# A three-layer transformer kernel: the first token tile's split moves into the output projection, and the first expert gather is cut in two

## The chip, the cores and the metric

The kernel runs on one core of a Trainium2 chip. The metric is the time of one execution on the device in microseconds (us). TensorE (PE) multiplies matrices, VectorE (DVE), ScalarE (ACT) and GpSimd (POOL) work on elements, and SyncE (SP) issues most of the transfers. Each engine works through its own instructions in the order in which the program issues them.

## The reference, cut to what matters

Three layers, each a token mixer and a mixture of experts, over 256 tokens of 1024 numbers in float32. The change lies between the mixer's output projection and the first expert product:

```python
x = x + gate1 * y                                  # y: the mixer's output projection
h = _rms(x, norm2_w[layer]) * (1 + scale2) + shift2
x = x + gate2 * _hier_moe(h, ...)

# in _hier_moe
g_sel = jnp.argmax(g_logits, axis=-1)              # 4 groups of 8 experts
top_v, top_i = lax.top_k(e_in, MOE_TOPK)           # 2 experts of the group
gate = (p_g * jax.nn.softmax(top_v, axis=-1)).reshape(-1)
def expert_block(args):
    tok, e = args
    xr = xt[tok]
    return (jax.nn.silu(xr @ w1[e]) * (xr @ w3[e])) @ w2[e]
```

The third layer's expert part is of the same kind, without shift, scale and gate. All 32 experts of a layer are computed, each for the tokens routed to it.

## The kernel before

The 256 tokens are two tiles of 128 (`t` = 0 and 1). All weights come through a ring of 18 slots of 1 MB. A plan fixes their order; `pump` issues the next transfer on SP while more slots are free than `self.reserve` holds back, `slot` takes one for data (and lowers the reserve by one), and `release` gives slots back, may raise the reserve, and pumps.

A mixer's last step is `out_last`: for each tile, two halves of 512 columns are projected on TensorE, and `out_sink` multiplies by the gate (first two layers) and adds to `x` on DVE, then ACT squares the half and sums it into `ssq`. While tile 1 is projected, tile 0 is transposed into `hT` (`route_turn`, copies on ACT and on DVE) and its router logits are multiplied (`route_logits`).

`moe` begins the routing. `x_rstd` sums `ssq` for both tiles at once, and `rstd` raises it to -0.5 on POOL. Then come `route_turn(1)` and `route_logits(1)`. ACT scales both tiles by `r` into `hh`, whose type float32r keeps the high part of each number. The low part `hl` is the scaled x less `hh`: for tile 0 POOL makes it in two steps (scaling into a scratch, then the subtraction), for tile 1 `rest` makes it in one DVE step.

`route` forms the logits `lg` and picks group and experts in a chain of small DVE steps, which ends with the mask `mk`. In the first two layers the late modulation products (`mods`) lie beside it on TensorE. `warm(n)` multiplies constants n times, only to keep TensorE busy. A product over `mk` counts ranks, `rk`. `onehot(0)` compares the ranks with 0 to 63 for four experts, `finish` makes the weights and the largest rank, and `gather(0)` multiplies `hh` and `hl` by the one-hot `u`, 256 columns for the two pairs 0 and 1 (two experts a pair); `affine` evacuates to `xg`, on ACT and DVE in turn. Every engine then reads the largest rank and branches around `overflow`.

The pairs follow: `up` with the first weights (`g`), `up` with the second (`u`), the turn, `down`, and `combine` of the pair before. After odd pairs the next two pairs are gathered.

Of the kernel before, what the change touches and what calls it, by code (L numbers as in the profile page):

```python
# [9 lines left out]
FT = mybir.dt.float32  # L10
# [9 lines left out]
P = 128  # L20
# [101 lines left out]
class Net:  # L122
# [396 lines left out]
    def out_last(self, act, gate):  # L519
        got = []  # L520
        setup = self.route_setup()
        next(setup)
        self.hT = self.slot().rearrange("p (k q) -> p k q", k=KC)
        for t in range(NT):
            for n in range(2):
                p = self.psum()
                for k2 in range(2):
                    i = 2 * n + k2
                    if i == len(got):
                        self.prep()  # L530
                        got.append(self.ready.pop(0))
                    wh, wl = got[i]
                    for k in range(2):
                        kk = 2 * k2 + k
                        self.mm3(p, tuple(x[:, P * t:P * t + P] for x in act[kk]), (wh[:, k], wl[:, k]), kk == 0, kk == 3)
                    yield (1.3, 0.0)
                self.out_sink(t, n, gate, True)(p)
                if not t and not n:
                    next(setup)
                if t:  # L540
                    (self.route_logits if n else self.route_turn)(0)
                    yield (1.8, 0.0)

# [124 lines left out]
    def gla(self, g, q):  # L668
# [116 lines left out]
        self.release(4, reserve=1)  # L785
# [83 lines left out]
    def even(self, coeffs):  # L869
# [91 lines left out]
        self.release(5, reserve=2)  # L961
# [16 lines left out]
    def odd(self, coeffs):  # L978
        nc, A, tc = self.nc, self.A, self.tc
        with tc.tile_pool(name="odd", bufs=1, reuse_waits="tile") as g:  # L980
# [77 lines left out]
            def stream():  # L1058
# [18 lines left out]
                self.release(3, reserve=1)  # L1077
# [4 lines left out]
        self.release(6, reserve=2)  # L1082
# [354 lines left out]
    def second(self, coeffs):  # L1437
        nc, tc = self.nc, self.tc
        with tc.tile_pool(name="sec", bufs=1, reuse_waits="tile") as g:
# [98 lines left out]
            def stream():  # L1538
# [23 lines left out]
                self.release(3, reserve=1)  # L1562
# [7 lines left out]
        self.release(6, reserve=2)  # L1570
# [58 lines left out]
    def route(self, g, r, mods, rest):  # L1629
# [5 lines left out]
        self.warm(1 if mods else 5)  # L1635
# [31 lines left out]
        rest()  # L1667
# [4 lines left out]
        self.warm(1)  # L1672
# [91 lines left out]
    def moe(self, l, mods, start, coeffs, slots, fill=None):  # L1764
        nc, tc = self.nc, self.tc
        _, w1, w3, w2, gate = self.moe_args(l)
        with tc.tile_pool(name="moe", bufs=1, reuse_waits="tile") as g:
            hT = self.hT
            hh, hl = (self.slot(FR).rearrange("p (t k q) -> p t k q", t=NT, k=KC) for i in range(2))
            r = self.x_rstd()  # L1770
# [3 lines left out]
            for t in range(NT):  # L1774
                nc.scalar.activation(hh[:, t], xv[:, t], AF.Copy, scale=r[:, t:t + 1])
            h0 = g.tile([P, KC, 2 * P], FT, name="xg").rearrange("p (t k) q -> p t (k q)", t=NT)[:, 0]
            h0 = h0.rearrange("p (k q) -> p k q", k=KC)
            nc.gpsimd.tensor_scalar(h0, xv[:, 0], r[:, 0:1], None, op0=OP.mult)
            nc.gpsimd.tensor_sub(hl[:, 0], h0, hh[:, 0].bitcast(FT))

            def rest():
                nc.vector.scalar_tensor_tensor(hl[:, 1], xv[:, 1], r[:, 1:2], hh[:, 1].bitcast(FT),
                                               op0=OP.mult, op1=OP.subtract)
# [20 lines left out]
            def gather(j):  # L1804
                xg = g.tile([P, KC, 2 * P], FT, name="xg")
                u = st["u", j].rearrange("p t a s -> p t (a s)")
                for k0 in range(0, KC, 2):
                    ps = self.psum().rearrange("p (k s) -> p k s", k=2)
                    for k in range(2):
                        for t in range(NT):  # L1810
                            for i, part in enumerate((hh, hl)):
                                self.mm(ps[:, k], part[:, t, k0 + k], u[:, t], t + i == 0, t + i == 2)
                    for k in range(2):
                        self.affine(xg[:, k0 + k], ps[:, k], k0 + k, "av"[k])
                st["xg"] = xg
# [108 lines left out]
            onehot(0)  # L1924
            finish()
            gather(0)
# [6 lines left out]
            for p in range(NP):  # L1933
# [13 lines left out]
                else:  # L1947
# [9 lines left out]
                    up(p, "u")  # L1957
                    if p % 2:
# [107 lines left out]
```

## Time and profile before

| | |
|---|---|
| median of 3 runs | 2107.69 us (2103.13 to 2118.58) |
| profiled execution, its own time | 2108.36 us |
| its span, first to last instruction | 2106.3 us |
| TensorE busy | 1901.6 us (90%) |
| DVE / ACT / POOL busy | 858.1 / 427.5 / 327.9 us |
| mean granted TensorE clock | 0.968 |
| read from memory | 722.48 MB, 344 GB/s over the span |

Times in the trace are counted from the span's start. A busy time is a sum over one engine and says nothing of what waits for what; for that the timeline is read around a wait. The granted clock is a share of 2.4 GHz. An arrow in square brackets gives an engine's idle time before an instruction and what ended it.

### The profile page before, as it was taken

What the parts mean: (1) busy time and instruction counts of PE and PEld (TensorE: products, weight loads), DVE (VectorE), ACT (ScalarE), POOL (GpSimd) and SP (SyncE); (2) the same over time, 40 slices, a digit from 0 to 9 for tenths busy, and PEclk for the clock granted to TensorE, in tenths of its full rate; (3) what the DMA queues carried; (4) which work ended last, traced back from release to release, by engine and by line L of the source; (5) the groups of instructions that cost most, each with busy time, mean ns of one, the idle gap of its engine ahead of it and who ended that gap; (6) DMA issues with size and microseconds to landing.
All of it is one profiled execution on the core that took longest, in us unless ns stands there. A gap on an engine that the chain in (4) does not pass through costs nothing. (4 is left out here: it accounts for less than half of the span.)

```text
span 2106.3 us, 24926 instructions
## 1 busy us (share of the span) xinstructions
PE 1901.6 (90%) x9930; PEld 1056.1 (50%) x9930; DVE 858.1 (41%) x1574; ACT 427.5 (20%) x778; POOL 327.9 (16%) x248
## 2 busy tenths in 40 slices
PE   6888799999999899899999999998899899999997
PEld 3656344444444667534444444586788344444443
DVE  3665333333322567533332232467666333232223
ACT  1423101111100343211110011254544111010011
POOL 1331100000000334100000000142444000000000
PEclk8998899999999999999999999998999999999999
DMA  9697799999999856799999999921357799999997
GB/s 323 238 319 297 260 422 421 422 421 421 421 421 406 300 222 244 294 365 421 421 421 421 421 421 421 326 101 41 125 194 300 292 421 421 421 421 422 421 421 285
DMA packets 157547, 725.35 MB, mean 344 GB/s; under 512 B 25305, under 2 KB 43088, under 8 KB 85226
## 3 DMA queue, kind: packets, MB, share of 16 engines
q1 hardware_dynamic: 139216, 716.84, 84.9%
q10 hardware_dynamic: 18201, 6.76, 1.3%
q8 instruction: 85, 1.39, 0.3%
q14 instruction: 45, 0.36, 0.0%
HBM read 722.48 MB, written 1.07 MB: 344 GB/s over the span
## 5 line engine op out<-in xcount | busy, mean ns | idle before, releaser
L257 PE MATMUL ps<-slot,xg 128*64 128x512 f32 x2992 | 710.5, 599 | 20.6 <-DMA slot<-moe_w 9.6
L257 PEld LDWEIGHTS ps<-slot,xg 128*64 128x64 f32 x2992 | 254.4, 138 | 422.0 <-issue 359.8
L257 PE MATMUL ps<-slot,ht 128*64 128x512 f32 (+1 forms) x1552 | 345.0, 574 | 56.4 <-issue 49.2
L257 PE MATMUL ps<-slot 128*128 128x256 f32 (+8 forms) x2230 | 368.4, 327 | 15.1 <-DVE slot L461 9.6
L257 PEld LDWEIGHTS ps<-slot 128*128 128x128 f32 (+3 forms) x2230 | 300.5, 187 | 73.6 <-issue 14.0
L257 PEld LDWEIGHTS ps<-slot,ht 128*64 128x64 f32 x1552 | 128.7, 139 | 228.4 <-issue 213.9
L1891 DVE TENSOR_TENSOR x<-x,ps 128x512 f32<-128x512 f32 x180 | 115.3, 682 | 277.0 <-PE ps L257 277.0
L1865 POOL TENSOR_TENSOR yl<-sg,yh 128x512 fp32r<-128x512 f32 (+1 forms) x68 | 82.5, 1213 | 884.8 <-ACT yh L1864 884.8
L462 POOL TENSOR_TENSOR slot<-slot 128x512 fp32r<-128x512 f32 (+2 forms) x108 | 164.4, 1539 | 273.2 <-ACT slot L460 261.9
L1844 DVE SCALAR_TENSOR_TENSOR hh<-sg,ws,ps 128x512 f32<-128x512 f32 x48 | 53.4, 1113 | 319.4 <-PE ps L257 179.8
L1864 ACT CAST yh<-sg 128x512 fp32r<-128x512 f32 (+1 forms) x68 | 40.3, 593 | 468.9 <-DVE sg L1863 468.9
L461 DVE TENSOR_TENSOR slot<-slot 128x512 fp32r<-128x512 f32 (+2 forms) x108 | 110.2, 1035 | 54.4 <-ACT slot L460 53.9
L1863 DVE TENSOR_TENSOR sg<-ps,ga 128x512 f32<-128x512 f32 (+1 forms) x68 | 44.9, 660 | 175.2 <-PE ps L257 175.2
L460 ACT CAST slot<-slot 128x1024 fp32r<-128x1024 f32 (+2 forms) x108 | 106.6, 1020 | 46.2 <-PE ps L257 27.3
L257 PEld LDWEIGHTS ps<-u,slot 128*128 128x128 f32 x768 | 96.9, 199 | 18.3 <-issue 17.0
L257 PE MATMUL ps<-u,slot 128*128 128x256 f32 x768 | 101.9, 293 | 0.0
L1840 ACT ACTIVATE sg<-ps 128x512 f32<-128x512 f32 x48 | 28.7, 598 | 312.4 <-PE ps L257 312.4
L257 PE MATMUL ps<-yh,pg 128*128 128x512 f32 (+1 forms) x204 | 87.1, 429 | 0.7 <-ACT yh L1864 0.7
L257 PE MATMUL ps<-yl,pg 128*128 128x512 f32 (+1 forms) x204 | 77.5, 382 | 0.9 <-POOL yl L1865 0.8
L1916 POOL TENSOR_TENSOR slot<-x,rows 128x512 f32<-128x512 f32 x2 | 2.5, 1272 | 464.5 <-DVE x L1912 464.5
L398 ACT ACTIVATE xg<-ps,cf 128x256 f32<-128x256 f32 x64 | 36.2, 565 | 156.6 <-PE ps L257 156.6
L1867 ACT CAST yh<-ps 128x512 fp32r<-128x512 f32 (+1 forms) x34 | 19.1, 561 | 227.3 <-PE ps L257 227.2
(334 smaller groups left out, 1586.4 us busy)
## 6 DMA issues: line engine op xcount, KB each, us to landing
slot<-moe_w SPq DMA_DIRECT2D x376, 1024.0 KB, 19.8
slot<-w_gate SPq DMA_DIRECT2D x59, 1024.0 KB, 17.7
slot<-w_up SPq DMA_DIRECT2D x59, 1024.0 KB, 19.8
slot<-w_down SPq DMA_DIRECT2D x50, 1024.0 KB, 18.1
slot<-ada_w SPq DMA_DIRECT2D x48, 1024.0 KB, 7.7
slot<-w_in SPq DMA_DIRECT2D x20, 1024.0 KB, 8.5
slot<-odd_w_in SPq DMA_DIRECT2D x12, 1024.0 KB, 13.1
more<-w_down SPq DMA_DIRECT2D x10, 1024.0 KB, 19.8
```

What stands on the lines that cost most here:

```text
L257: self.nc.tensor.matmul(out, lhsT=lhsT, rhs=rhs, start=start, stop=stop)
L398: self.nc.scalar.activation(out, p, AF.Identity, scale=a, bias=nb[:, k:k + 1])
L460: nc.scalar.copy(wh, src)
L461: nc.vector.tensor_sub(wl[:, 0], src[:, 0], wh[:, 0].bitcast(FT))
L462: nc.gpsimd.tensor_sub(wl[:, 1], src[:, 1], wh[:, 1].bitcast(FT))
L1840: nc.scalar.activation(sg, ps, AF.Silu)
L1844: nc.vector.scalar_tensor_tensor(ha.rearrange("s k p -> s p k"), st["sg", p].rearrange("s (p k) -> s p k", k=4), st["ws", p], ps.rearrange ...
L1863: nc.vector.tensor_mul(y, ps, self.ga[:, sl])
L1864: nc.scalar.copy(yh, y)
L1865: nc.gpsimd.tensor_sub(yl, y, yh.bitcast(FT))
L1867: nc.scalar.copy(yh, ps)
L1891: nc.vector.tensor_add(self.x[:, t, sl], self.x[:, t, sl], ps)
```

## The change

A new `token_split(t)` is called in `out_last` after each tile's second half. It sums and raises the tile's own `ssq`, scales the tile into `hh` on ACT, and for tile 0 makes `hl` on POOL, with the part of `hT` that belongs to tile 1 as scratch. `moe` no longer does this; its `x_rstd`, both scalings and the POOL steps are gone. The two slots for `hh` and `hl` are taken at the start of `out_last`, and the reserves are raised before it and dropped after it accordingly (five places; the hunks left out are of the kind shown). `rest` makes the low part of tile 1 in two halves, one at its old place and one after `onehot(0)`. The first gather makes only the 128 columns of pair 0; those of pair 1 follow after pair 0's second `up`. `warm` goes from 5 to 7 (layer 2) after the logits and from 1 to 2 after the rank product.

```diff
--- before.py
+++ after.py
@@ -521,6 +521,8 @@
         setup = self.route_setup()
         next(setup)
         self.hT = self.slot().rearrange("p (k q) -> p k q", k=KC)
+        self.hs = [self.slot(FR).rearrange("p (t k q) -> p t k q", t=NT, k=KC) for i in range(2)]
+        self.hr = self.cp.tile([P, NT], FT, name="xr", bufs=2)
         for t in range(NT):
             for n in range(2):
                 p = self.psum()
@@ -537,9 +539,24 @@
                 self.out_sink(t, n, gate, True)(p)
                 if not t and not n:
                     next(setup)
+                if n:
+                    self.token_split(t)
                 if t:
                     (self.route_logits if n else self.route_turn)(0)
                     yield (1.8, 0.0)
+
+    def token_split(self, t):
+        nc = self.nc
+        r = self.hr[:, t:t + 1]
+        nc.vector.tensor_reduce(r, self.ssq[:, t, :2], axis=AX.X, op=OP.add)
+        self.rstd(r, r, D)
+        hh, hl = self.hs
+        xv = self.x[:, t].rearrange("q (p k) -> q k p", k=KC)
+        nc.scalar.activation(hh[:, t], xv, AF.Copy, scale=r)
+        if t == 0:
+            f = self.hT[:, :, P:]
+            nc.gpsimd.tensor_scalar(f, xv, r, None, op0=OP.mult)
+            nc.gpsimd.tensor_sub(hl[:, t], f, hh[:, t].bitcast(FT))
 
     def plan_cols(self, key, w, c0, n):
         src = w.rearrange("(p k) n -> p k n", k=KC)[:, :, c0:c0 + n]
@@ -782,7 +799,7 @@
                        p.rearrange("p (h q) -> p h q", h=4))
             yield (0.9, 0.0)
         self.flag("ob", 1.5)
-        self.release(4, reserve=1)
+        self.release(4, reserve=3)
 
     def swa(self, g, bias, sc):
         nc, A = self.nc, self.A
@@ -1632,7 +1649,7 @@
         for t in range(NT):
             nc.vector.scalar_tensor_tensor(lg[:, t], self.lp[:, t], r[:, t:t + 1], self.br, op0=OP.mult, op1=OP.add)
         late = self.mods(mods[0][0], mods[0][1], (0, 1)) if mods else None
-        self.warm(1 if mods else 5)
+        self.warm(1 if mods else 7)
         gl = lg[:, :, 0:4]
         el = lg[:, :, 4:36]
 
@@ -1664,12 +1681,12 @@
         ob = g.tile([P, NT, 8], FT, name="ob")
         nc.vector.tensor_add(ob, o1, o2)
         nc.vector.tensor_mul(v4(mk), gb, r4(ob))
-        rest()
+        rest(0)
         p = self.psum((P, NT, E))
         self.mm(p[:, 0], self.ltri, mk[:, 0], True, True)
         self.mm(p[:, 1], self.ones, mk[:, 0], True, False)
         self.mm(p[:, 1], self.ltri, mk[:, 1], False, True)
-        self.warm(1)
+        self.warm(2)
         rk = g.tile([P, NT, E], FT, name="rk")
         nc.vector.scalar_tensor_tensor(rk, p, 1.0, mk, op0=OP.add, op1=OP.mult)
         nc.vector.tensor_scalar(rk, rk, -1.0, None, op0=OP.add)
@@ -1766,21 +1783,14 @@
         _, w1, w3, w2, gate = self.moe_args(l)
         with tc.tile_pool(name="moe", bufs=1, reuse_waits="tile") as g:
             hT = self.hT
-            hh, hl = (self.slot(FR).rearrange("p (t k q) -> p t k q", t=NT, k=KC) for i in range(2))
-            r = self.x_rstd()
+            hh, hl = self.hs
+            r = self.hr
             self.route_turn(1)
             self.route_logits(1)
             xv = self.x.rearrange("q t (p k) -> q t k p", k=KC)
-            for t in range(NT):
-                nc.scalar.activation(hh[:, t], xv[:, t], AF.Copy, scale=r[:, t:t + 1])
-            h0 = g.tile([P, KC, 2 * P], FT, name="xg").rearrange("p (t k) q -> p t (k q)", t=NT)[:, 0]
-            h0 = h0.rearrange("p (k q) -> p k q", k=KC)
-            nc.gpsimd.tensor_scalar(h0, xv[:, 0], r[:, 0:1], None, op0=OP.mult)
-            nc.gpsimd.tensor_sub(hl[:, 0], h0, hh[:, 0].bitcast(FT))
-
-            def rest():
-                nc.vector.scalar_tensor_tensor(hl[:, 1], xv[:, 1], r[:, 1:2], hh[:, 1].bitcast(FT),
-                                               op0=OP.mult, op1=OP.subtract)
+            def rest(k):
+                nc.vector.scalar_tensor_tensor(hl[:, 1, k:k + 4], xv[:, 1, k:k + 4], r[:, 1:2],
+                                               hh[:, 1, k:k + 4].bitcast(FT), op0=OP.mult, op1=OP.subtract)
 
             rk, wt, ti, finish, late = self.route(g, r, mods, rest)
             NP = E // 2
@@ -1801,18 +1811,19 @@
                 nc.vector.tensor_mul(uw, u, bc(wt, 2 * p, 2))
                 st["uw", p] = uw
 
-            def gather(j):
-                xg = g.tile([P, KC, 2 * P], FT, name="xg")
+            def gather(j, c=slice(0, 2 * P)):
+                if c.start == 0:
+                    st["xg"] = g.tile([P, KC, 2 * P], FT, name="xg")
+                xg = st["xg"]
                 u = st["u", j].rearrange("p t a s -> p t (a s)")
                 for k0 in range(0, KC, 2):
-                    ps = self.psum().rearrange("p (k s) -> p k s", k=2)
+                    ps = self.psum().rearrange("p (k s) -> p k s", k=2)[:, :, :c.stop - c.start]
                     for k in range(2):
                         for t in range(NT):
                             for i, part in enumerate((hh, hl)):
-                                self.mm(ps[:, k], part[:, t, k0 + k], u[:, t], t + i == 0, t + i == 2)
+                                self.mm(ps[:, k], part[:, t, k0 + k], u[:, t, c], t + i == 0, t + i == 2)
                     for k in range(2):
-                        self.affine(xg[:, k0 + k], ps[:, k], k0 + k, "av"[k])
-                st["xg"] = xg
+                        self.affine(xg[:, k0 + k, c], ps[:, k], k0 + k, "av"[k])
 
             def gather_w(p):
                 ps = self.psum((P, T))
@@ -1922,8 +1933,9 @@
                 add(3)
 
             onehot(0)
+            rest(4)
             finish()
-            gather(0)
+            gather(0, slice(0, P))
             if late is not None:
                 late()
             self.pump()
@@ -1955,6 +1967,8 @@
                             nc.scalar.dma_start(fw, self.A["final_norm_2"].rearrange("(o n) -> o n", o=1)
                                                 .to_broadcast([P, D]))
                     up(p, "u")
+                    if not p:
+                        gather(0, slice(P, 2 * P))
                     if p % 2:
                         gather(p // 2 + 1)
                         if p == NP - 3:
```

## Rows read from the trace of the kernel before

**Rows 1.** Windows by stretch: length, busy time of each engine, granted clock, DMA share, rate.

```profile
core 0: us, PE busy (x) PEld busy (x) DVE busy (x) ACT busy (x) POOL busy (x), PEclk, DMA share, GB/s
220.00:225.00 5.00, 4.42 (x20) 4.00 (x21) 2.87 (x16) 0.95 (x4) 0.00 (x0) 0.50 0.70 290
225.00:230.00 5.00, 2.28 (x16) 2.08 (x15) 3.01 (x6) 1.72 (x4) 0.00 (x0) 0.84 0.04 10
250.00:260.00 10.00, 8.30 (x40) 2.83 (x38) 2.46 (x5) 0.00 (x0) 0.00 (x0) 1.00 0.81 252
300.00:400.00 100.00, 93.99 (x462) 41.30 (x460) 32.76 (x50) 10.61 (x18) 7.67 (x6) 1.00 1.01 421
```

**Rows 2.** Timeline of layer 0's routing: start, length, engine, line, operation.

```profile
201.45 0.19 ACT L382 ACTIVATION_READ_ACCUMULATOR junk<-x 128x1 f32 x1
...
206.50 0.69 DVE L508 TENSOR_TENSOR x<-x,junk 128x512 f32<-128x512 f32 x1
...
207.99 0.59 ACT L248 COPY slot<-ps 128x512 f32<-128x512 f32 x1
208.04 0.16 DVE L387 TENSOR_REDUCE xr<-ssq 128x2 f32<-128x4 f32 x1 [0.85 <-ACT junk L382]
...
208.48 0.70 POOL L378 TENSOR_TENSOR xr<-xr,mhalf 128x2 f32<-128x2 f32 x1 [15.81 <-DVE xr L377]
...
208.63 1.98 PE L257 MATMUL ps<-wr,slot 128*128 128x36 f32 x16 [0.23 <-ACT slot L248]
209.21 4.22 ACT L1775 ACTIVATE slot<-x,xr 128x1024 fp32r<-128x1024 f32 x2 [0.63 <-POOL xr L378]
209.28 3.87 POOL L1778 TENSOR_SCALAR xg<-x,xr 128x1024 f32<-128x1024 f32 x1
...
210.53 3.64 PE L257 MATMUL ps<-slot,condz 128*32 128x512 f32 x32
210.71 0.42 DVE L1633 SCALAR_TENSOR_TENSOR lg<-ps,xr,br 128x36 f32<-128x36 f32 x2 [1.58 <-PE ps L257]
...
213.23 2.35 POOL L1779 TENSOR_TENSOR slot<-xg,slot 128x1024 fp32r<-128x1024 f32 x1
...
217.25 2.06 DVE L1782 SCALAR_TENSOR_TENSOR slot<-x,xr,slot 128x1024 fp32r<-128x1024 f32 x1
...
221.09 6.19 PE L257 MATMUL ps<-u,slot 128*128 128x256 f32 x32
...
231.44 9.40 PE L257 MATMUL ps<-slot,xg 128*64 128x512 f32 x32 [4.15 <-issue]
```

**Rows 3.** Timeline of layer 1: the first gather and the first expert product.

```profile
871.05 5.54 PE L257 MATMUL ps<-u,slot 128*128 128x256 f32 x32
...
879.37 7.09 PE L257 MATMUL ps<-slot,xg 128*64 128x512 f32 x32 [2.78 <-DVEq L1717]
```

**Rows 4.** Timeline of layer 2's routing.

```profile
1617.72 0.18 ACT L382 ACTIVATION_READ_ACCUMULATOR junk<-x 128x1 f32 x1
...
1625.68 1.98 PE L257 MATMUL ps<-wr,slot 128*128 128x36 f32 x16 [0.23 <-ACT slot L248]
...
1627.49 4.24 PE L257 MATMUL ps<-km 128*128 128x476 f32 x10
...
1638.04 5.99 PE L257 MATMUL ps<-u,slot 128*128 128x256 f32 x32
...
1645.85 7.09 PE L257 MATMUL ps<-slot,xg 128*64 128x512 f32 x32 [1.82 <-DVEq L1717]
```

**Rows 5.** One source line's instructions: shortest, median and longest in ns.

```profile
L1649 DVE TENSOR_TENSOR oh<-km,i x6: 174/176/2083, 213.5 to 1633.6; 128x16 f32<-128x16 f32 x6
```

**Rows 6.** Timeline of TensorE over pairs 0 and 1 of layer 0.

```profile
252.97 0.66 PE L267 MATMUL ps<-km,hh 128*128 128x128 f32 x4 [0.91 <-DVE hh L1844]
...
276.43 4.00 PE L257 MATMUL ps<-u,slot 128*128 128x256 f32 x32
```

**Rows 7.** Groups by shape from 1345 to 1385 us on TensorE: count, busy us.

```profile
L257 PE MATMUL ps<-slot 128*128 128x152 f32 x36 | 4.5, 274 | 0.0
```

**Rows 8.** The branch around the overflow code on TensorE's sequencer, in ns.

```profile
L1717 PEldq COMPARE_BRANCH  x3: 3578/3798/3818, 224.9 to 1641.6; - x3
```

More of the change, by code (lines that the diff above doesn't have):

```diff
@@ L960, in even @@
                        stream())
-        self.release(5, reserve=2)
+        self.release(5)
     def plan_odd(self):
@@ L1076, in stream @@
                 yield tuple(("o", h) for h in range(4, 8))
-                self.release(3, reserve=1)
+                self.release(3, reserve=3)
                 yield from self.out_last([(self.o[0][:, h], self.o[1][:, h]) for h in range(4, 8)], True)
@@ L1081, in odd @@
             self.weave(*[transposed(s) for s in (2, 0, 3, 1)], *[head(h) for h in range(8)], stream())
-        self.release(6, reserve=2)
+        self.release(6)
     def plan_second(self):
@@ L1561, in stream @@
                 yield from branch(self.o[2:], 1)
-                self.release(3, reserve=1)
+                self.release(3, reserve=3)
                 coeffs()
@@ L1569, in second @@
             self.weave(self.nsa_prep(g), self.nsa_attn(g, sc), self.hgrn(g, q8), stream())
-        self.release(6, reserve=2)
+        self.release(6)
     def plan_moe(self, l):
```

## The prediction

> **What bounds the kernel now.** I read the windows by stage first. In the expert stages the weight stream and TensorE are both nearly full: between 300 and 400 us TensorE works 94 of 100 us while the DMA engines move 421 GB/s without a gap [rows 1]. So nothing can be won inside such a stage; what can move are its two ends. The start is visible in the same view: from 225 to 230 us the DMA engines move 10 GB/s, because the ring is full and TensorE has not yet used a weight, and from 250 to 260 us they are again below their rate, because the ring is still full before the first pair's last product [rows 1]. A microsecond by which TensorE's first products, up to the `down` of pair 0, come earlier or later therefore moves the weight stream and TensorE together, and the stage with them. The routing stretch in front of each of the three expert stages is what this change edits, so next I read that stretch in order of time, for all three layers [rows 2 to 4], and ask at each step what it waited for.
>
> In layer 0 the chain is: the last squared sum, two short DVE steps, POOL's power at 208.48, then beside it the second tile's transposes with a copy on ACT at 207.99 and the logits at 208.63; `lg` at 210.71; a chain of small DVE steps; the first gather at 221.09; the first expert product at 231.44 [rows 2]. In that DVE chain one 16-element step takes 2.08 us where the median of its kind is 0.18 [rows 5]; it starts at 213.5, under POOL's 2.35 us subtraction [rows 2], and that stall is what the change can take away.
>
> **The change part by part.** The terms are later (+) or earlier (-) per layer, as layer 0 / 1 / 2. Layer 1 repeats layer 0's times up to the gather, so layer 0's rows serve for both.
>
> *Second tile's logits, a loss.* The new `token_split(1)` is issued inside `out_last`, so on ACT the second tile's scaling into `hh` now stands in front of the ACT copy of `route_turn(1)`. Before, that copy came at 207.99 and the scalings after it, from 209.21 [rows 2]. Now ACT must wait for the second power, and that stands on POOL behind the first tile's two steps. Layer 0: the first tile's sum is read by 201.64; sum and power start take 0.44 (208.04 to 208.48), the power 0.70, POOL's scaling 3.87, its subtraction 2.35: with small gaps POOL is free at 209.2, or 209.55 if the subtraction waits for the DVE add that ends at 207.19 [rows 2]. Then the power 0.70, half of ACT's 4.22 us pair of scalings, 2.11, and the copy, 0.59, end at 212.7 to 213.0, and the logits, which need that copy, start there instead of at 208.63 [rows 2]: +4.1 to +4.45, taken +4.3. DVE's half of the copy also waits for the subtraction, which reads the scratch in `hT`, but ends long before ACT's. Layer 2 begins at 1617.90: POOL is free at 1625.4, the copy ends at 1628.95 against logits at 1625.68 [rows 4]: +3.3. Queued behind this wait on TensorE are the late modulation products (layers 0 and 1) or the clock-keeping ones (layer 2), on DVE everything from `lg` on.
>
> *POOL's subtraction out of the DVE chain, a gain.* 2.08 less 0.18 us [rows 5]: -1.9 each, since the subtraction is now over by 209.6, before `lg`.
>
> *The low half of tile 1 in two pieces.* The 2.06 us step [rows 2] stood whole between the mask and the ranks; now about 1.03 stands there and 1.03 between the one-hot and `finish`'s maximum. The gather stands behind that maximum's product on TensorE, so it waits for both halves as before. Taken 0; ends -1.0 (all of one half hidden) and +0.3 (the rank step no longer hides in it).
>
> *TensorE between logits and ranks.* The DVE chain from `lg` at 210.71 to the end of the mask, just before 217.25, is now 6.5 - 1.9 = 4.6 us. TensorE has about as much in that time: in layers 0 and 1 the 3.64 us of modulation and one clock-keeping product [rows 2]; in layer 2 seven instead of five, 4.24 x 7 / 5 = 5.9 us [rows 4], some 1.0 us too long. The second `warm` after the ranks lies beside the rank, one-hot and half-step work. But TensorE now stands idle for about 3.5 us, from the second tile's transposes to its logits. In the stretch of before, after a shorter gap, the granted clock was 0.50 from 220 to 225 us, the 1.2 GHz level, and the gather took 6.19 us against 4.00 us at the 2.4 GHz level [rows 1, 2, 6]. If it falls here too, logits and modulation take up to twice as long: 0 to +2.3 in layers 0 and 1, +1 to +4 in layer 2. Which it will be no row decides, so I take +1.2 / +1.2 / +2.0.
>
> Sum up to the start of the gather: 4.3 - 1.9 + 1.2 = +3.6, the same in layer 1, and 3.3 - 1.9 + 2.0 = +3.4.
>
> *From the gather to the first expert product, a gain.* This takes 231.44 - 221.09 = 10.35, 8.32 and 7.81 us [rows 2 to 4]. Half the columns buy little: products of 152 columns take 4.5 us / 36 = 125 ns [rows 7], and the gather's of 256 columns take 4.00 us / 32 = 125 ns [rows 6], so at the high clock the time is that of the weight loads, whose number stays 32. The saving is that of the clock, if TensorE is busy from logits to gather and keeps or regains 2.4 GHz: 6.19, 5.54 and 5.99 us [rows 2 to 4] towards 4.00, and in layer 0 also the first product group, 9.40 instead of 7.09. Against it stands TensorE's own branch around the overflow code, 3.6 to 3.8 us [rows 8], which no faster gather shortens; layer 2, without the late DVE add, is already close to that. Ends: 0 to -5.7 / -1.5 / -1.3; taken -2.4 / -1.0 / -0.8.
>
> *The second half of the first gather, a loss.* It is another 32 products, 4.00 us [rows 6], now between pair 0's `u` product and its turn. It covers the 0.91 us in which TensorE waited for `hh` at the turn at 252.97 [rows 6]: 4.00 - 0.91 = +3.1, ends +2.9 (the wait for the turned copy covered as well) and +4.0. It delays `down` of pair 0, which follows that turn, just where the ring is still full [rows 1], so the stream is delayed as well. In layer 2 the stream is longer at its rate by then; +2.3, lower end +1.5.
>
> *The reserves.* Two ring slots are held from `out_last` on instead of from the routing on, so two 1 MB transfers come later, some 5 us at 421 GB/s [rows 1]. The cover is the time in which the ring is full before the first product, nearly all of 225 to 230 in layer 0 [rows 1]: 0. Without that cover it would be up to +5.
>
> Sum: layer 0 is 3.6 - 2.4 + 3.1 = +4.3; layer 1 is 3.6 - 1.0 + 3.1 = +5.7; layer 2 is 3.4 - 0.8 + 2.3 = +4.9: together +14.9. The profiled execution took 2108.36 us (span 2106.3), 0.7 above the median of 2107.69, so the forecast is 2107.7 + 14.9, about 2122 us. All lower ends together give about +3, all upper ends about +27; ends of one kind in all three layers are unlikely, so the forecast's own range is 2113 to 2130.
>
> **The rivals.** *First, ACT is not in the way, and the change is faster.* If the second power is ready early enough that ACT scales tile 1 before the transposes are done, the logits stay at their time: 0 - 1.9 + 0 - 2.4 + 3.1 = -1.2, then 0.2 in layer 1 and -0.4 in layer 2, about 2106; and if the second half of the gather hides as well, some 8.5 less, about 2098. It decides at one point: POOL's subtraction must end before about 205.2 us in layer 0's time, which is a power and a scaling, 0.70 and 2.11 us, ahead of the copy at 207.99 [rows 2]. For it speaks only that POOL's spans are rough; against it that its three steps alone add up to 6.9 us, from 202.1.
>
> *Second, DVE loses the race with POOL, and it is clearly slower.* POOL's subtraction now runs beside the projection. It should start about 206.8, and the DVE add of the last quarter of x starts at 206.50 [rows 2]: 0.3 us decide. If POOL is first, that add, with both inputs in SBUF like the step that was stretched to 2.08 [rows 5], ends about 2.3 us later, and with it the second tile's transposes and sum, in layers 0 and 1 (in layer 2 the add reads PSUM): +4.4 in all, about 2127, and up to 2132 where the longer gap also costs the clock. The Trainium skill's page "SBUF — State Buffer", section "Who interferes with whom", states this case as a rule: a DVE instruction with two SBUF inputs and a GpSimd one that reads SBUF exclude each other, and whichever issues first holds the port to its end. The stretched step of 2.08 us agrees; that rule alone would also let POOL's 3.87 us scaling stop such DVE steps, which no row here shows.
>
> *Third, the second half of the gather is hidden.* If the weight stream at 421 GB/s alone sets the end of a stage and its last pause lies before `down` of pair 0, the term of 8.5 falls away: 2122 - 8.5, about 2114. For it speaks the stream without a gap; against it the pause between 250 and 260 us [rows 1].
>
> **How the numbers follow.** Forecast 0.55, first rival 0.18, second 0.14, third 0.13. The range is 2102 to 2131: the forecast's own, all of the third rival, most of the second and the slower half of the first. About one per cent, 21 us, is what a measurement of this kernel can tell from no change. Faster by more than that, under 2087, is in none of the cases with any weight: 0.03. Slower by more, over 2129, is half of the second rival and the upper end of the forecast: 0.18. Between them 0.79.
>
> **What would show it.** Right: in layer 0 the ACT order square, scaling of tile 1, copy; the second tile's logits 4 us after their place of before; no DVE step of 16 elements over 1 us; 32 products from `u` at pair 0 twice, each near 4 us; `down` of pair 0 several us later against the end of the projection. A low granted clock over the logits and the modulation would show the upper ends, a high one over the gather the lower. Wrong: a copy of tile 1 that ACT does before the scaling; a quarter-of-x add of over 2 us (the second rival); a stage whose end doesn't move although its `down` of pair 0 does (the third).

## The result, and the profile after

The changed kernel takes 2124.96 us (median of 11 runs, 2120.77 to 2130.88) where the kernel before took 2110.89 beside it (11 runs): ratio 1.0076, interval 1.0065 to 1.0088. That is 0.8% slower: +14.1 us between the medians, +16.0 by the ratio; the forecast was +14.9. The profiled execution has a span of 2122.9 us against 2106.3, +16.6, and a mean granted clock of 0.964 against 0.968. The figure is right and, as the runs below show, the path to it is not.

The timeline of layer 0's routing after the change (start, length, engine, line, operation) answers to [rows 2]:

```profile
202.67 2.36 ACT L555 ACTIVATE slot<-x,xr 128x1024 fp32r<-128x1024 f32 x1 [1.04 <-POOL xr L378]
...
202.74 4.10 POOL L558 TENSOR_SCALAR slot<-x,xr 128x1024 f32<-128x1024 f32 x1
202.85 2.80 DVE L508 TENSOR_TENSOR x<-x,junk 128x512 f32<-128x512 f32 x1
...
206.88 0.69 DVE L508 TENSOR_TENSOR x<-x,junk 128x512 f32<-128x512 f32 x1
206.93 2.86 POOL L559 TENSOR_TENSOR slot<-slot 128x1024 fp32r<-128x1024 f32 x1
206.99 2.10 PE L257 MATMUL ps<-wr,slot 128*128 128x36 f32 x16 [1.26 <-ACT slot L248]
...
208.90 1.95 PE L267 MATMUL ps<-km,x 128*128 128x128 f32 x8
...
210.36 2.14 ACT L555 ACTIVATE slot<-x,xr 128x1024 fp32r<-128x1024 f32 x1 [1.97 <-POOL xr L378]
...
212.40 0.56 ACT L248 COPY slot<-ps 128x512 f32<-128x512 f32 x1
213.10 3.60 PE L257 MATMUL ps<-wr,slot 128*128 128x36 f32 x16 [2.26 <-ACT slot L248]
216.63 6.45 PE L257 MATMUL ps<-slot,condz 128*32 128x512 f32 x32
...
223.92 0.75 PE L257 MATMUL ps<-mk,km 128*128 128x32 f32 x6
...
227.42 3.79 PE L257 MATMUL ps<-u,slot 128*128 128x128 f32 x32
...
234.04 9.73 PE L257 MATMUL ps<-slot,xg 128*64 128x512 f32 x32 [2.83 <-DVE uw L1811]
```

Read downwards: ACT's order is the one forecast (scaling at 210.36, copy at 212.40, logits at 213.10 instead of 208.63). One thing was not forecast. POOL's scaling, in front by 0.11 us, goes with a DVE add at 202.85 that takes 2.80 us instead of 0.69. The copies of tile 0's transposes stand behind that add, so tile 0's logits start 1.4 us later than before and tile 1's transposes 1.6 us later. The next add, at 206.88, is 0.05 us ahead of POOL's subtraction and keeps its 0.69. Another thing was held possible only: the logits and the modulation, 1.98 and 3.64 us in [rows 2], take 3.60 and 6.45. Tile 1's transposes, in front of them, take 1.95 us. Before they took 1.12 (timeline of TensorE):

```profile
207.27 1.12 PE L267 MATMUL ps<-km,x 128*128 128x128 f32 x8
```

The windows of the same execution show the clock behind this, and answer to [rows 1] (after the engines' busy times: granted clock, DMA share, GB/s):

```profile
core 0: us, PE busy (x) PEld busy (x) DVE busy (x) ACT busy (x) POOL busy (x), PEclk, DMA share, GB/s
205.00:210.00 5.00, 3.74 (x26) 3.28 (x25) 2.85 (x6) 1.95 (x6) 4.92 (x3) 0.87 1.00 374
210.00:215.00 5.00, 2.74 (x13) 2.37 (x13) 0.69 (x1) 2.60 (x2) 0.32 (x1) 0.50 1.00 423
215.00:220.00 5.00, 5.00 (x24) 2.36 (x28) 2.78 (x16) 0.00 (x0) 0.00 (x0) 0.50 0.27 74
...
225.00:230.00 5.00, 4.23 (x29) 3.03 (x28) 4.19 (x19) 1.23 (x4) 0.00 (x0) 1.00 0.99 406
...
235.00:240.00 5.00, 5.00 (x16) 1.65 (x14) 0.00 (x0) 0.00 (x0) 0.00 (x0) 0.56 0.56 195
...
300.00:400.00 100.00, 94.62 (x459) 40.30 (x456) 31.35 (x47) 10.13 (x17) 10.22 (x8) 1.00 1.01 421
```

From 210 to 220 us, while TensorE stands before the late logits and then works through them, the granted clock is 0.50, the 1.2 GHz level. In this layer it falls before ACT's wait begins: it is 1.00 until 208 us and 0.50 from 209 on, under tile 1's transposes, behind the wait of 1.26 us in front of tile 0's logits (206.99). It is back at 1.00 for the gather, and low again (0.56) under the first expert product. From 300 us on the stage is as before.

One line's instructions, shortest, median and longest in ns: the 16-element DVE step of [rows 5], now L1666, and TensorE's branch of [rows 8], now L1734.

```profile
L1666 DVE TENSOR_TENSOR oh<-km,i x6: 174/175/176, 219.6 to 1650.0; 128x16 f32<-128x16 f32 x6
...
L1734 PEldq COMPARE_BRANCH  x3: 3594/3903/4171, 229.7 to 1658.6; - x3
```

The 2.08 us step is gone, as forecast, and the branch is about as long as it was.

Layer 1 up to the first `down` (TensorE and ACT; ACTq is ACT's queue with its own transfer issues) answers to [rows 3]:

```profile
886.38 9.54 PE L257 MATMUL ps<-slot,xg 128*64 128x512 f32 x32 [2.86 <-DVE uw L1811]
...
899.68 7.09 PE L257 MATMUL ps<-slot,xg 128*64 128x512 f32 x32
...
901.26 4.62 ACTq L1611 DMA_DIRECT2D br<-b_grp  x1
...
906.70 3.79 PE L257 MATMUL ps<-u,slot 128*128 128x128 f32 x32
...
913.93 0.34 ACTq L1148 DMA_DIRECT2D ll<-hg_lb_logits  x1
914.32 1.51 ACT L398 ACTIVATE xg<-ps,cf 128x128 f32<-128x128 f32 x4 [13.89 <-DMA k_causal<-k_causal]
...
917.63 7.56 PE L257 MATMUL ps<-slot,ht 128*64 128x512 f32 x24 [6.46 <-issue]
```

The first product takes 9.54 us instead of 7.09. The second half of the gather (906.70) is over at 910.5, but ACT does not evacuate its share before 914.32: it has been issuing transfers since 899.86, one of them for 4.62 us. `down` starts 17.95 us after the second `up`. Before, it was 9.81:

```profile
890.22 7.09 PE L257 MATMUL ps<-slot,xg 128*64 128x512 f32 x32
...
900.03 7.09 PE L257 MATMUL ps<-slot,ht 128*64 128x512 f32 x32 [0.78 <-DVE ht L250]
```

Layer 2 (timeline of TensorE) answers to [rows 4]:

```profile
1642.33 3.60 PE L257 MATMUL ps<-wr,slot 128*128 128x36 f32 x16 [3.36 <-ACT slot L248]
...
1662.72 8.78 PE L257 MATMUL ps<-slot,xg 128*64 128x512 f32 x32 [2.35 <-PEq L1734]
```

### The profile page after: what moved, and what is told of

Its sections match the earlier page's. It is cut to its first block, busy times and chain, and to the rows that moved or that the text cites. A ratio compares the mean times of both kernels' runs of the same rounds, so it can differ in the third digit from the quotient of the medians.

```text
span 2122.9 us, 25176 instructions
## 1 busy us (share of the span) xinstructions
PE 1915.2 (90%) x10036; PEld 1063.4 (50%) x10036; DVE 860.5 (41%) x1595; ACT 432.0 (20%) x790; POOL 330.3 (16%) x251
## 5 line engine op out<-in xcount | busy, mean ns | idle before, releaser
L257 PEld LDWEIGHTS ps<-slot,xg 128*64 128x64 f32 x2992 | 248.1, 138 | 413.2 <-issue 375.1
L1902 DVE TENSOR_TENSOR x<-x,ps 128x512 f32<-128x512 f32 x180 | 115.3, 683 | 270.0 <-PE ps L257 270.0
L257 PEld LDWEIGHTS ps<-u,slot 128*128 128x128 f32 x864 | 101.7, 189 | 20.1 <-issue 20.1
L257 PE MATMUL ps<-u,slot 128*128 128x256 f32 (+1 forms) x864 | 106.9, 281 | 0.0
L398 ACT ACTIVATE xg<-ps,cf 128x256 f32<-128x256 f32 (+1 forms) x72 | 38.4, 542 | 173.2 <-PE ps L257 148.5
```

The lines of the kernel that those rows point to most:

```text
L257: self.nc.tensor.matmul(out, lhsT=lhsT, rhs=rhs, start=start, stop=stop)
L398: self.nc.scalar.activation(out, p, AF.Identity, scale=a, bias=nb[:, k:k + 1])
L1902: nc.vector.tensor_add(self.x[:, t, sl], self.x[:, t, sl], ps)
```

## The experiments

There were twelve runs, each timed beside the kernel before. Microseconds are the ratio less 1, times 2108. The last two columns come from each run's profiled execution: the start of pair 0's second `up` and of pair 0's first `down`, counted from the start of tile 0's transposes, summed over the three layers, less the same sum of before (115.3 and 144.7; layer 0 of before gives 42.67 and 52.48). They are of one execution each, whose own time lies up to 7 us from the median of its run (run 1).

| run | what | ratio, interval | us | second `up` | `down` |
|---|---|---|---|---|---|
| - | changed kernel | 1.0076 (1.0065 to 1.0088) | +16.0 | +13.9 | +30.2 |
| 1 | changed, ACT's old order | 1.0025 (1.0009 to 1.0042) | +5.3 | +3.4 | +18.3 |
| 2 | changed, whole gather | 1.0070 (1.0053 to 1.0086) | +14.8 | +13.1 | +13.5 |
| 3 | 1 and 2 | 1.0012 (0.9999 to 1.0026) | +2.5 | +3.0 | +3.3 |
| 4 | before, gather cut | 1.0046 (1.0032 to 1.0060) | +9.7 | +7.9 | +24.3 |
| 5 | changed, DVE evacuates | 1.0035 (1.0021 to 1.0050) | +7.4 | +14.1 | +23.4 |
| 6 | changed, old clock-keeping | 1.0074 (1.0049 to 1.0099) | +15.6 | +16.0 | +31.0 |
| 7 | 3, clock kept behind the gather | 0.9994 (0.9979 to 1.0009) | -1.3 | -2.1 | -1.7 |
| 8 | before, ACT's new order | 1.0036 (1.0019 to 1.0053) | +7.6 | +8.5 | +8.5 |
| 9 | 1 and 5 | 0.9999 (0.9985 to 1.0013) | -0.2 | +3.4 | +12.7 |
| 10 | 9, clock kept behind the gather | 0.9986 (0.9974 to 0.9998) | -3.0 | -0.3 | +9.0 |
| 11 | 4, DVE evacuates | 1.0042 (1.0029 to 1.0054) | +8.9 | +7.9 | +17.2 |
| 12 | 11, clock kept throughout | 0.9963 (0.9950 to 0.9977) | -7.8 | -7.9 | +1.4 |

**Runs 1 to 4: each part undone, and the cut alone.** Run 1 puts tile 1's scaling behind the copies of `route_turn(1)`:

```diff
-        nc.scalar.activation(hh[:, t], xv, AF.Copy, scale=r)
         if t == 0:
+            nc.scalar.activation(hh[:, t], xv, AF.Copy, scale=r)
...
             xv = self.x.rearrange("q t (p k) -> q t k p", k=KC)
+            nc.scalar.activation(hh[:, 1], xv[:, 1], AF.Copy, scale=r[:, 1:2])
```

> The change, with one step put back: the second tile's scaling into the high parts is issued on ScalarE behind the copies of its transposes, as it was before. Theory (the order on ScalarE makes the second tile's logits late, and the gap costs TensorE's clock): in layer 0 these logits come back from 213.1 to about 210 or 211 us (VectorE's half of the copy still waits for GpSimd's subtraction), the modulation products take about 3.6 us again instead of 6.5, the first gather starts near 223 instead of 227.4, and the time falls by 5 to 9 us, to about +7 us against the kernel before. Rival (all of the loss is the second half of the first gather, the weight stream hides the start): the logits come back, the time stays at +14 us.

Run 2 keeps the first gather whole, and run 3 has both edits:

```diff
-            gather(0, slice(0, P))
+            gather(0)
...
-                    if not p:
-                        gather(0, slice(P, 2 * P))
```

> The change, but the first gather makes all 256 columns at once, as before. Theory (the second half costs its 32 products and, where ScalarE's queue is held by the transfers that it issues for the next layer, also the wait for its evacuation): the gap between the second expert product and the first down product of layer 1 falls from 10.9 us to about 2.7 us; the start of each stage stays late by 3 to 6 us; the time falls by 6 to 11 us, to about +4 us. Rival (the late start is the whole loss, the weight stream hides what comes behind it): the gap falls, the time stays within 3 us of +14.

> The change with both steps put back: ScalarE scales the second tile behind the copies, and the first gather is whole. What is left of the change is the first tile's early split, the second tile's low part in two pieces, the reserves and the clock-keeping products. Theory: GpSimd's subtraction no longer stretches a small VectorE step by 1.9 us in the routing chain, but it now lies beside the projection; about -2 us against before, between -5 and +2. Rival (the early GpSimd steps or the reserves are the loss): +5 us or more.

Run 4 is the kernel before with the new `gather(j, c)` and its two calls, nothing else.

> The kernel before with one part of the change alone: the first gather in two halves, the second behind pair 0's second expert product. Theory (32 more products of 3.8 us, and ScalarE's evacuations held behind the transfers it issues): the gap before the first down product grows by 3 to 8 us by layer, of which the weight stream hides a part; +5 us against before, between +3 and +9. Rival (the second half is hidden by the weight stream): within 2 us of before. Rival (half a gather lets the first product start earlier, which pays): -3 us or less.

Measured: ACT's order alone is worth 10.7 us (+16.0 to +5.3), the cut 1.2 us beside the rest (+16.0 to +14.8) and 2.8 without ACT's order (run 1 against run 3); for the cut the intervals overlap both times. But alone, on the kernel before, the cut costs 9.7. The parts don't add. In run 4 the first half of the gather runs wholly at the low level, 7.09 us for 128 columns in all three layers, where the whole gather took 6.19, 5.54 and 5.99 [rows 2 to 4]. In run 1, layer 0's second logits start at 8.65 us after tile 0's transposes, against 11.18 in the changed kernel and 6.70 before: undoing ACT's order gives back 2.5 of the 4.5 us, and the rest remains, beside the stretched DVE add (2.77 us there). The expectation had the modulation back at 3.6 us; in layer 0 it takes 6.06, and the clock is low there with ACT out of the way too (timeline of run 1, TensorE, layer 0):

```profile
207.65 1.93 PE L267 MATMUL ps<-km,x 128*128 128x128 f32 x8
209.46 3.63 PE L257 MATMUL ps<-wr,slot 128*128 128x36 f32 x16
```

In layers 1 and 2 of run 1 the logits take 1.97 and 1.98 us, against 2.79 and 3.60 in the changed kernel. So in these two the low clock came with ACT's order, and in layer 0 it was there already, behind the stretched add. (Behind that add it can go either way: in run 7, with the same order on ACT, layer 0's logits take 1.98 us and layer 1's 3.63.) Run 2's expectation of +4 failed and its rival held: nearly the whole loss is there without the cut. Run 3 came out above the expected -2, run 4 just above the upper end of +9.

**Runs 5 and 6: the evacuation, and the clock-keeping products.** Run 5 takes ACT out of the second half's evacuation; run 6 has `warm` back at 5 and 1.

```diff
-                        self.affine(xg[:, k0 + k, c], ps[:, k], k0 + k, "av"[k])
+                        self.affine(xg[:, k0 + k, c], ps[:, k], k0 + k, "v" if c.start else "av"[k])
```

```diff
-        self.warm(1 if mods else 7)
+        self.warm(1 if mods else 5)
...
-        self.warm(2)
+        self.warm(1)
```

> The change, but the second half of the first gather is evacuated by VectorE alone; nothing of it stands in ScalarE's queue. Theory (these evacuations waited behind the transfers that ScalarE issues for the next layer): in layer 1 the time from the start of the second expert product to the down product falls from 17.95 to about 13 us, as in layer 2, in layer 0 from 14.8 to about 13; since the weight stream hides part of it, the time falls by 1 to 5 us, to about +11 us against before. Rival (the wait is for the products or for VectorE itself): the 17.95 us stay, and the time with them.

> The change with the numbers of clock-keeping products as before (5 in layer 2, 1 after the rank product). Theory (seven of them hold TensorE past the mask in layer 2): the rank product of layer 2 comes about 2 us earlier, the time is 1 to 3 us less than the change's, about +12 us against before. Rival (they keep the granted clock): the gather takes 5 to 6 us again instead of 3.8 and the time is the change's or more.

Timeline of run 5 in layer 1: the end of ACT's transfers, and `down`.

```profile
912.47 0.30 ACTq L1148 DMA_DIRECT2D ll<-hg_lb_logits  x1
...
912.78 7.09 PE L257 MATMUL ps<-slot,ht 128*64 128x512 f32 x32 [1.45 <-issue]
```

ACT's transfers still run to 912.77, 12.9 us behind the second `up` (14.6 in the changed kernel), but DVE has evacuated by 911.4: `down` comes 12.94 us after the second `up` instead of 17.95, and the median gains 8.6 us on the changed kernel. So ACT's queue was a cost, and one that no step of the prediction had. How much of the 8.6 it was, the traces leave open: from tile 0's transposes in layer 1 to those in layer 2, run 5 takes 3.1 us less than the changed kernel, and the other two stages agree within 0.4; the profiled execution of run 5 is the longest of its twelve.

Run 6 gains nothing, but its timeline (TensorE, layer 0) shows what the added products do:

```profile
226.16 7.05 PE L257 MATMUL ps<-u,slot 128*128 128x128 f32 x32
```

Without them the gather starts 1.6 us sooner in layers 0 and 2, and takes 7.05 / 5.84 / 6.26 us instead of 3.79: what they delay they give back.

**Runs 7 and 8: the clock behind the gather, and ACT's order alone.** Run 7 adds three clock-keeping groups between gather and branch to run 3; run 8 is the kernel before with tile 1 scaled ahead of `route_turn(1)` and tile 0 behind `route_logits(1)`.

```diff
             gather(0)
+            self.warm(3)
```

```diff
             r = self.x_rstd()
+            xv = self.x.rearrange("q t (p k) -> q t k p", k=KC)
+            nc.scalar.activation(hh[:, 1], xv[:, 1], AF.Copy, scale=r[:, 1:2])
             self.route_turn(1)
             self.route_logits(1)
-            xv = self.x.rearrange("q t (p k) -> q t k p", k=KC)
-            for t in range(NT):
-                nc.scalar.activation(hh[:, t], xv[:, t], AF.Copy, scale=r[:, t:t + 1])
+            nc.scalar.activation(hh[:, 0], xv[:, 0], AF.Copy, scale=r[:, 0:1])
```

> The kernel of the third experiment (tile 1 scaled behind its copies, the gather whole) with three clock-keeping products more, behind the first gather, where TensorE waits for the branch. Theory (a fast gather only lengthens the idle time before the branch, and the clock falls over the first expert product, which took 9 to 10 us in place of 7.1): the first expert product takes 7.1 us in at least two layers; the time is 3 to 6 us less than the third experiment's, about -2 us against before. Rival (the products put TensorE's branch off by their own time): the first expert product starts 1 to 2 us later and nothing is won: +2 us or more.

> The kernel before with one step moved: ScalarE scales the second tile in front of the copies of its transposes, and the first tile behind. Nothing else of the change. Theory (the order on ScalarE alone makes the loss): the second tile's logits start about 3.4 us later (power, scaling 2.1 us, copy 0.6 us), TensorE's clock falls in the gap in some layers, and the time is +7 us against before, between +4 and +11. Rival (what is late there is made up before the first expert product): within 2 us of before.

Timeline and windows of run 8, layer 0: ACT's scaling, its copy, the logits; then the clock.

```profile
212.26 2.13 ACT L1772 ACTIVATE slot<-x,xr 128x1024 fp32r<-128x1024 f32 x1 [1.20 <-POOL xr L378]
...
214.29 0.57 ACT L248 COPY slot<-ps 128x512 f32<-128x512 f32 x1
...
214.91 3.54 PE L257 MATMUL ps<-wr,slot 128*128 128x36 f32 x16 [3.47 <-ACT slot L248]
```

```profile
core 0: us, PE busy (x) PEld busy (x) DVE busy (x) ACT busy (x) POOL busy (x), PEclk, DMA share, GB/s
210.00:215.00 5.00, 1.53 (x14) 1.34 (x13) 1.26 (x4) 3.47 (x5) 3.37 (x2) 1.00 0.65 269
215.00:220.00 5.00, 5.00 (x24) 3.71 (x28) 1.27 (x7) 1.95 (x1) 3.51 (x2) 0.50 0.00 0
```

Nothing but the order on ACT has been changed here, and it costs 7.6 us: the logits wait 3.47 us, start 3.2 us later in layers 0 and 1 (2.5 in layer 2), and take 3.54 instead of 1.98, with the clock at 0.50 from 215 us on, right behind the wait. In run 7 the first product takes 7.09 us in all layers (10.08 and 9.63 in layers 0 and 1 of run 3), and the time is that of before; against run 3 the intervals overlap.

**Runs 9 to 11: do the causes add, and what did the cut cost alone?** Run 9 joins the edits of 1 and 5, run 10 adds `warm(3)` behind the first half of the gather, and run 11 is run 4 with the evacuation of run 5.

> The changed kernel with two things undone: tile 1 is scaled into hh behind the copies of route_turn(1), and the second half of the first gather is evacuated by DVE alone. If the two causes are separate (ACT's order was worth 10.7 us, ACT's transfer issues ahead of the evacuation 6.6), the time is the first run's +5.3 less 6.6, about -1 us: ratio 0.998 to 1.001. If the first run had already hidden most of the evacuation's delay under the weight stream, little is left to gain: ratio 1.001 to 1.0025. In the trace either way: layer 1's stretch from the second up to down of pair 0 falls from 16.6 to about 13 us.

> As the run before, with three clock-keeping groups behind the first half of the gather, where TensorE otherwise waits for the branch. If the low clock over the first expert product (9.3 to 9.7 us instead of 7.1) is a cost that the stage keeps, the time falls by 2 to 5 us against the run before: ratio 0.996 to 0.999. If the weight stream sets the stage once the first products are late, the trace shows the product at 7.1 us and the time stays within 2 us of the run before.

> The kernel before with the cut of the first gather alone, as in the fourth run, but its second half evacuated by DVE alone. If what the cut cost there (+9.7 us) was mostly ACT's transfer issues ahead of the evacuation, 6 us go: ratio 1.001 to 1.003, and the stretch from the second up to down of pair 0 in layer 1 falls from 18.1 to about 13 us. If it was the gather's low clock (7.09 us for 128 columns) and the late first product, the ratio stays at 1.0035 to 1.005.

Run 9 came out where separate causes would have it: 5.5 us below run 1 by the medians, with intervals that overlap a little. The two traces do not show it: each of the three stages is the same in them within 0.2 us. Run 10 is 2.8 us faster still; the two intervals overlap, so the direction is likely and no more. Run 11 went against the evacuation: `down` in layer 1 comes 12.94 us after the second `up` instead of 18.14, and the time stays (1.0042 against 1.0046). The windows and the timeline (TensorE) of run 11, layer 0:

```profile
core 0: us, PE busy (x) PEld busy (x) DVE busy (x) ACT busy (x) POOL busy (x), PEclk, DMA share, GB/s
...
225.00:230.00 5.00, 5.00 (x25) 5.00 (x25) 2.09 (x12) 1.01 (x3) 0.00 (x0) 0.50 0.37 154
230.00:235.00 5.00, 1.57 (x8) 1.38 (x7) 2.52 (x5) 1.88 (x3) 0.00 (x0) 0.50 0.04 10
```

```profile
224.48 7.09 PE L257 MATMUL ps<-u,slot 128*128 128x128 f32 x32
...
235.22 9.79 PE L257 MATMUL ps<-slot,xg 128*64 128x512 f32 x32 [3.65 <-DVE uw L1801]
```

The gather and the first half of the first product run at the low level (0.50, up to 240 us), and the weight stream stands (10 GB/s) until the first product. So the clock was the suspect.

**Run 12: the cut with the clock kept.** Run 11 with more clock-keeping:

```diff
-        self.warm(1 if mods else 5)
+        self.warm(3 if mods else 7)
...
-        self.warm(1)
+        self.warm(2)
...
             gather(0, slice(0, P))
+            self.warm(3)
```

> The run before (cut of the first gather, its second half evacuated by DVE) with more clock-keeping groups around it: three instead of one after the logits (seven instead of five in layer 2), two instead of one after the ranks, three behind the first half of the gather. If the low clock is what the cut cost there, the gather takes 3.8 instead of 7.09 us, the first expert product 7.1 instead of 9.1 to 10.0, and the ratio falls from 1.0042 to 0.998 to 1.0015. If the cost is the late second half and a weight stream that starts late, the products are short and the ratio stays above 1.0025.

Windows and timeline (TensorE) of run 12, layer 0:

```profile
core 0: us, PE busy (x) PEld busy (x) DVE busy (x) ACT busy (x) POOL busy (x), PEclk, DMA share, GB/s
...
220.00:225.00 5.00, 4.77 (x36) 4.15 (x37) 3.26 (x19) 2.13 (x6) 0.00 (x0) 1.00 0.63 259
225.00:230.00 5.00, 3.79 (x15) 1.49 (x15) 1.97 (x4) 1.28 (x1) 0.00 (x0) 1.00 0.26 59
230.00:235.00 5.00, 5.00 (x24) 1.73 (x20) 0.00 (x0) 0.00 (x0) 0.00 (x0) 1.00 0.85 292
```

```profile
220.54 3.79 PE L257 MATMUL ps<-u,slot 128*128 128x128 f32 x32
...
227.99 7.09 PE L257 MATMUL ps<-slot,xg 128*64 128x512 f32 x32 [1.21 <-PEq L1717]
...
245.86 3.79 PE L257 MATMUL ps<-u,slot 128*128 128x128 f32 x32
...
251.78 7.09 PE L257 MATMUL ps<-slot,ht 128*64 128x512 f32 x32 [1.45 <-issue]
```

The granted clock is 1.00 in every 5 us window from 205 to 240, gather and first product take 3.79 and 7.09 us in all three layers, and the kernel takes 2100.69 us against 2108.08: ratio 0.9963, the fastest of all and below the range that had been expected (0.998). That is 16.7 us below run 11, from clock-keeping products alone, with the second half of the gather still at pair 0.

## Why the prediction was right, and where only its sum was

Each term as forecast and as measured in the profiled executions (layers 0 / 1 / 2):

- *Second tile's logits*: +4.3 / +4.3 / +3.3 forecast, +4.5 / +4.5 / +3.1 measured. The chain on POOL and ACT came as worked out (in layer 0 the copy ends at 212.96, forecast 212.7 to 213.0), but it is half of the cause. Undoing ACT's order gives back 2.5 to 2.7 (changed kernel less run 1); in layers 0 and 1 the other 1.8 to 2.0 remain in run 1, where the add beside POOL's scaling is stretched. Layer 2, whose add reads PSUM, has 0.5 left.
- *POOL's subtraction out of the DVE chain*: right; all six steps take 174 to 176 ns. *Low half in two pieces*: right; from ranks to gather 3.50 us, before 3.62 to 3.71.
- *TensorE between logits and ranks*: +1.2 / +1.2 / +2.0 forecast. From the logits to the ranks it took 10.82 / 9.65 / 10.75 us, before 8.84 / 8.85 / 8.65; with the 1.9 won on DVE that makes +3.9 / +2.7 / +4.0, at or over the upper ends. The low clock that the prediction thought possible came in every layer, in layer 0 ahead of ACT's wait, which it named, and behind the stretched add.
- *From the gather to the first product*: -2.4 / -1.0 / -0.8 forecast, -3.7 / -1.7 / -1.7 measured. But the product itself, 9.40 / 7.09 / 7.09 before, took 9.73 / 9.54 / 8.78. The prediction kept the clock for the gather and did not ask who keeps it behind the gather. (Its lower end for layer 0, -5.7, is more than its rows give: 2.2 for the gather and 2.3 for the first product make 4.5.)
- *Second half of the first gather*: +3.1 / +3.1 / +2.3 forecast; from the second `up` to `down` it took 5.0 / 8.1 / 3.2 us longer. What was missing is a queue: ACT evacuates half of it, and ACT stood in its own transfer issues (until 914.32 in layer 1). In layer 2, where DVE's evacuation brings almost nothing (12.8 us from `up` to `down` in run 5, 13.0 in the changed kernel), the term is close, 0.9 above.
- *The reserves*: right, though not tried alone. In the changed kernel the stream stands again before the first product of every layer (12, 4 and 8 GB/s in the two microseconds before it), so the two slots held early took nothing from it.

Added up to `down` of pair 0 this is +7.9 / +14.0 / +8.2, together +30.2, twice the forecast, but the span grew by 16.6. Stage by stage, from tile 0's transposes in one layer to those in the next (in layer 2 to the end), it grew by +3.6 / +10.0 / +3.1; the second `up` came +2.9 / +5.9 / +5.1 later. So the step that failed is the first one, in the reading of the stage: that each microsecond "up to the `down` of pair 0" moves the stream and with it the stage. The runs say how far it holds. In layer 1 of run 1 `down` comes 9.4 us later than before, the second `up` 2.6, and the stage is 0.1 us longer. Run 2 has its `down` 16.7 us earlier than the changed kernel and is 1.2 us faster; run 12 has its `down` 1.4 us later than before and is 7.8 faster. The start of the second `up` goes with the median time within 3 us in ten of the twelve runs and in the changed kernel. Taken against the span of the very execution that was profiled it is off by up to 7.4 us, and `down` by up to 22.3; part of that is the stretch ahead of layer 0's routing, which in runs 4, 8, 11 and 12 is the code of before and lasts from 0.4 us less to 3.6 us more.

That the stream is released over the first product fits: it stands until that product in run 11 and runs at 292 GB/s behind its start in run 12. No run moved that point alone, so this is argued, not shown. The third rival, with the second half of the gather hidden, was thus right on its point for the most part, given 0.13; layer 1, with +10.0 where the second `up` has +5.9, is the exception, and run 5 brings it to +6.9. Two errors cancelled: too little for the clock and ACT's queue, and too much for the second half. That the sum came so near is luck. The forecast's own working had no way to tell the errors apart; only the runs have. The prediction also held that a change under about one per cent cannot be told from none; the interval here is 0.12% to either side.

The second rival's race was won by DVE by 0.05 us in layer 0 (206.88 against 206.93), and in layer 1 likewise (860.34 against 860.39). But its mechanism came one add earlier, under the 4.10 us scaling (in layer 1 too, 2.78 us). The prediction had said of just this that no row shows it.

The Trainium skill's page "SBUF — State Buffer", section "Who interferes with whom", had it: a DVE instruction with two SBUF inputs contends with a GpSimd one that reads SBUF, over ports that are an exclusive lock. The trace agrees on the delay, but not on its length: the add ended at 205.65, more than a microsecond before the 206.84 at which POOL's scaling is shown to end.

What the early split costs with the rest put right can be bounded from runs 10 and 12. They differ in it (with the reserves and the low half in two pieces), and in that run 10 has one clock-keeping group after the logits of layers 0 and 1 where run 12 has three: -3.0 against -7.8 us, so some 5 us for all this together, with intervals that just touch. In the traces 3.4 us of it lie in layer 0, where run 10 has the add stretched and the clock at 0.50 from 215 to 220 us, and none in layer 1.

Open: why the evacuation by DVE gained 8.6 and 5.5 us by the medians in runs 5 and 9 and nothing in run 11, while the traces have 3.1 us of it in layer 1 of run 5 and nothing in run 9. Runs 5 and 9 are also those that the second `up` explains least (by 6.7 and 3.6 us), and they speak against the reading that nothing behind it counts. Whether ACT's scaling, which began with POOL's, has a part in the stretched add. And whether run 12 needs the cut: the whole gather with all its clock-keeping was not run. In run 7, with the whole gather, the first product starts 8.04 / 7.49 / 7.18 us after the gather does, in run 12 7.45 / 7.45 / 6.64, so the cut may be worth half a microsecond in layers 0 and 2 and the clock the rest.

## What to carry to other kernels

Work that is put on an in-order engine ahead of a copy on the path can cost its whole wait, and then the clock of what stands behind it (in run 8, 3.2 us and 1.6 us of a layer's logits); list for each moved step what its engine has queued, transfer issues too. Before moving work out of a routing gap, fill the gap: here clock-keeping products beside a DVE wait and a branch moved more time (16.7 us between runs 11 and 12) than any reordering won. And find the point at which a delayed stage is really released, by shifting things on either side of it, before counting delays up to a later one.

## What the runs showed of the hardware

A gather of 128 columns is hardly faster than one of 256 at the high level (3.79 against 4.00 us for 32 products), and at the low level it took 7.09 us in all three layers of runs 4 and 11, without the clock coming back during it. ACT's issue of one small transfer took 4.62 us in layer 1 of the changed kernel and another 7.10 in layer 0 (at 248.40), and in layer 1 a row of them stood in front of the engine's arithmetic for 14 us. Beside POOL's scaling a DVE add of 512 columns with two SBUF inputs took 2.80 us instead of 0.69, while in the kernel before DVE steps of 8 and 16 columns with two inputs took 0.17 to 0.18 beside the same scaling (211.36, 212.92).
